# Mean-centred squares on one core: four 4 MB loads on one queue and stores on another, changed to two 8 MB loads with row-by-row computation and all stores on the loads' queue

## The chip, the cores and the metric

One core of one Trainium2 chip runs the program; the other cores are idle. The metric is the device time of one execution in microseconds, given as the median of several runs. A profile's own span is some 1.8 us shorter than this time (82.9 against 84.65 us before the change), so spans are compared with spans and times with times.

## The reference

```python
def reference(x, axis):                 # x: 1024 x 4096 float32, axis -1
    mean = np.mean(x, axis=axis, keepdims=True)
    return ((x - mean) ** 2).astype(np.float32)
```

Every row needs its whole mean before its first output can be computed. 16.78 MB are read and 16.78 MB written.

## The kernel before

The 1024 rows are four tiles of 128 partitions with two rows each. All four tiles have their own buffer, so no load ever waits for one.

Some terms. DVE (VectorE) sums the rows and ACT (ScalarE) squares them; SP (SyncE) computes nothing here and only issues transfers (DMAs). A transfer goes into the queue of the engine that issues it, and both queues use the same 16 DMA engines. A *run* is the contiguous stretch that a transfer moves for one partition: 32 KiB for two rows, 64 KiB for four. A *packet* is one record of a DMA engine in the profile; apart from small ones, here it is one run. The *turn* is the moment when the loads end and the stores take over.

```python
Q = 2
x_t = x.rearrange("(n p q) d -> n p (q d)", p=P, q=Q)
out_t = out.rearrange("(n p q) d -> n p (q d)", p=P, q=Q)
for i in range(ntiles):                                   # 4 tiles
    x_tile = pool.tile([P, Q * D], mybir.dt.float32)
    nc.sync.dma_start(out=x_tile, in_=x_t[i])             # L40: SP's queue, 32 KiB per partition
    x_tiles.append(x_tile)
for i in range(ntiles):
    x_tile = x_tiles[i].rearrange("p (q d) -> p q d", q=Q)
    # ... neg_sum, neg_mean: [P, Q] ...
    nc.vector.reduce_sum(out=neg_sum, in_=x_tile, axis=X, negate=True)            # L47
    nc.vector.tensor_scalar_mul(out=neg_mean, in0=neg_sum, scalar1=inv_d)         # L53
    for q in range(Q):
        nc.scalar.activation(out=x_tile[:, q, :], in_=x_tile[:, q, :],
                             func=Square, bias=neg_mean[:, q:q + 1], scale=1.0)   # L56
    nc.scalar.dma_start(out=out_t[i], in_=x_tiles[i])     # L63: ACT's queue
```

(Cuts: imports, the pools, the launch.) A scheduler fixes the order of each engine's instructions at build time, and it need not be the order of the source.

## Time and profile before

| | before |
|---|---|
| time, median | 84.65 us |
| span of the profile | 82.9 us |
| DVE, ACT busy | 43%, 37% of the span |
| packets of the two DMA queues, share of 16 engines' span | 48.6% + 47.0% |
| bytes over the span | 405 GB/s |

How to read it: the last two rows say that the 16 DMA engines are the bound. The packets themselves took 95.6% of 82.9 us, which is 79.25 us; in the other 3.65 us an average DMA engine had no packet.

The groups of instructions of the kernel before (columns: busy us and mean ns of one, then idle time ahead of them and what ended it) show where the two arithmetic engines stand:

```profile
L47 DVE TENSOR_REDUCE neg_sum<-x_tile 128x2 f32<-128x8192 f32 x4 | 34.7, 8686 | 25.6 <-DMA x_tile<-in_x_dram 25.6
L56 ACT ACTIVATE x_tile<-x_tile,neg_mean 128x4096 f32<-128x4096 f32 x8 | 29.2, 3700 | 24.9 <-DVE neg_mean L53 24.9
```

Both are idle for about 25 us while they wait for data or for each other. Neither is the bound.

### The profile page before, as it was taken

To read this page: it belongs to the slowest core of one execution; us is meant where nothing else is said; L and a number is where in the kernel's file an instruction comes from. 1 tells how busy PE (TensorE), PEld (TensorE's weight loads), DVE (VectorE), ACT (ScalarE), POOL (GpSimd) and SP (SyncE) were. 2 spreads that over 40 slices of the span, in tenths; PEclk is the share of its full clock that TensorE was granted. 3 is DMA by queue.
4 is the path that set the end of the run, shared out by engine and by line. 5 is a ranking of instruction groups with operands and counts; after the bars stand their busy time and mean duration, and the time that the engine had idled before them with its cause. 6 is when DMAs were issued, how large, how long until landed. Compare 5 with 4: busy or idle time off the path is not lost.

```text
span 82.9 us, 75 instructions
## 1 busy us (share of the span) xinstructions
DVE 35.4 (43%) x8; ACT 30.5 (37%) x9; POOL 0.2 (0%) x4
## 2 busy tenths in 40 slices
DVE  0000007999599995999900000799950000000000
ACT  0000006000399917998099950000049990000000
POOL 0000000000000000000000000000000000000000
DMA  7779997997999899997997999899796996995990
GB/s 190 300 332 443 506 427 332 506 490 316 459 506 411 348 506 285 443 474 316 490 490 332 443 490 427 348 506 474 332 443 285 506 490 269 506 506 253 506 506 0
DMA packets 1153, 33.55 MB, mean 405 GB/s; under 512 B 129, under 2 KB 129, under 8 KB 129
## 3 DMA queue, kind: packets, MB, share of 16 engines
q1 hardware_dynamic: 576, 16.78, 48.6%
q10 hardware_dynamic: 576, 16.78, 47.0%
q14 instruction: 1, 0.00, 0.0%
HBM read 16.78 MB, written 16.78 MB: 405 GB/s over the span
## 4 chain that ended last, share of the span: by engine, by line
DMA 37%; DVE 21%; another core or an unknown queue 13%; ACT 5%; issue 4%; SPq 1%
DMA x_tile<-in_x_dram 37%; DVE neg_sum L47 21%; ACT x_tile L56 5%; SPq L40 1%; DVE neg_mean L53 0%
## 5 line engine op out<-in xcount | busy, mean ns | idle before, releaser
L47 DVE TENSOR_REDUCE neg_sum<-x_tile 128x2 f32<-128x8192 f32 x4 | 34.7, 8686 | 25.6 <-DMA x_tile<-in_x_dram 25.6
L56 ACT ACTIVATE x_tile<-x_tile,neg_mean 128x4096 f32<-128x4096 f32 x8 | 29.2, 3700 | 24.9 <-DVE neg_mean L53 24.9
L56 ACT ACT_TABLE_LOAD x1 | 1.3, 1283 | 13.1 <-DMA x_tile<-in_x_dram 13.1
L53 DVE TENSOR_SCALAR neg_mean<-neg_sum 128x2 f32<-128x2 f32 x4 | 0.7, 170 | 0.1
L80 POOL MEMSET const-bfloat16-1.0<- 128x1 bf16 x1 | 0.1, 102 | 0.0
L80 POOL MEMSET const-uint8-127<- 128x1 uint8 x1 | 0.1, 102 | 0.0
L80 POOL MEMSET const-float32-1.0<- 128x1 f32 x1 | 0.1, 99 | 0.0
L80 POOL MEMSET const-float32-0.0<- 128x1 f32 x1 | 0.1, 98 | 0.2 <-issue 0.2
## 6 DMA issues: line engine op xcount, KB each, us to landing
x_tile<-in_x_dram SPq DMA_DIRECT2D x4, 4096.0 KB, 26.2
out_dram<-x_tile ACTq DMA_DIRECT2D x4, 4096.0 KB, 17.4
```

Source lines behind the costliest of these rows:

```text
L40: nc.sync.dma_start(out=x_tile, in_=x_t[i])
L47: nc.vector.reduce_sum(out=neg_sum, in_=x_tile, axis=mybir.AxisListType.X, negate=True,)
L53: nc.vector.tensor_scalar_mul(out=neg_mean, in0=neg_sum, scalar1=inv_d)
L56: nc.scalar.activation(out=x_tile[:, q, :], in_=x_tile[:, q, :], func=mybir.ActivationFunctionType.Square, bias=neg_mean[:, q:q + 1], scal ...
L80: nc = _bacc.Bacc("TRN2", target_bir_lowering=False, num_devices=1)
```

## The change

Its intent: fewer and longer loads (64 KiB per partition instead of 32), outputs that leave two rows at a time so that a large tile need not be finished before its first store, and one issuing queue, SP's, for everything.

```diff
-    Q = 2
+    Q = 4
+    H = 2
...
     for i in range(ntiles):                 # 2 tiles now
         for q in range(Q):
-        nc.vector.reduce_sum(out=neg_sum, in_=x_tile, ...)        # both rows at once
-        nc.vector.tensor_scalar_mul(out=neg_mean, in0=neg_sum, scalar1=inv_d)
-        for q in range(Q):
-            nc.scalar.activation(..., bias=neg_mean[:, q:q + 1])
-        nc.scalar.dma_start(out=out_t[i], in_=x_tiles[i])
+            row = tiles[i][:, q * D:(q + 1) * D]
+            nc.vector.reduce_sum(out=neg_sum, in_=row, ...)        # one row
+            nc.vector.tensor_scalar_mul(out=neg_mean, in0=neg_sum, scalar1=inv_d)
+            nc.scalar.activation(out=row, in_=row, ..., bias=neg_mean)
+            if q % H == H - 1:
+                part = slice((q + 1 - H) * D, (q + 1) * D)
+                nc.sync.dma_start(out=out_t[i][:, part], in_=tiles[i][:, part])
```

(Condensed; the loads' code is the same with Q = 4. H is the number of rows per store.)

More of the change, by code (lines that the diff above doesn't have):

```diff
@@ L10 @@
 from concourse._compat import with_exitstack
+F32 = mybir.dt.float32
 @with_exitstack
@@ L32 @@
     out_t = out.rearrange("(n p q) d -> n p (q d)", p=P, q=Q)
-    pool = ctx.enter_context(tc.tile_pool(name="io", bufs=ntiles))
-    stats = ctx.enter_context(tc.tile_pool(name="stats", bufs=ntiles))
-    x_tiles = []
+    io = ctx.enter_context(tc.tile_pool(name="io", bufs=ntiles))
+    stats = ctx.enter_context(tc.tile_pool(name="stats", bufs=2 * ntiles * Q))
+    tiles = []
     for i in range(ntiles):
-        x_tile = pool.tile([P, Q * D], mybir.dt.float32)
+        x_tile = io.tile([P, Q * D], F32)
         nc.sync.dma_start(out=x_tile, in_=x_t[i])
-        x_tiles.append(x_tile)
+        tiles.append(x_tile)
     for i in range(ntiles):
-        x_tile = x_tiles[i].rearrange("p (q d) -> p q d", q=Q)
-        neg_sum = stats.tile([P, Q], mybir.dt.float32)
-        neg_mean = stats.tile([P, Q], mybir.dt.float32)
-        nc.vector.reduce_sum(
-            out=neg_sum,
-            in_=x_tile,
-            axis=mybir.AxisListType.X,
-            negate=True,
-        )
-        nc.vector.tensor_scalar_mul(out=neg_mean, in0=neg_sum, scalar1=inv_d)
-        for q in range(Q):
+        for q in range(Q):
+            row = tiles[i][:, q * D:(q + 1) * D]
+            neg_sum = stats.tile([P, 1], F32)
+            neg_mean = stats.tile([P, 1], F32)
+            nc.vector.reduce_sum(
+                out=neg_sum, in_=row, axis=mybir.AxisListType.X, negate=True
+            )
+            nc.vector.tensor_scalar_mul(out=neg_mean, in0=neg_sum, scalar1=inv_d)
             nc.scalar.activation(
-                out=x_tile[:, q, :],
-                in_=x_tile[:, q, :],
+                out=row,
+                in_=row,
                 func=mybir.ActivationFunctionType.Square,
-                bias=neg_mean[:, q:q + 1],
+                bias=neg_mean,
                 scale=1.0,
             )
-        nc.scalar.dma_start(out=out_t[i], in_=x_tiles[i])
+            if q % H == H - 1:
+                part = slice((q + 1 - H) * D, (q + 1) * D)
+                nc.sync.dma_start(out=out_t[i][:, part], in_=tiles[i][:, part])
 _INS = ['x', 'axis']
```

## The prediction

> **What bounds the kernel now.** I read the page top down: busy shares, then the DMA row and the queues.
>
> ```profile
> DVE 35.4 (43%) x8; ACT 30.5 (37%) x9; POOL 0.2 (0%) x4
> ...
> DMA  7779997997999899997997999899796996995990
> ...
> q1 hardware_dynamic: 576, 16.78, 48.6%
> q10 hardware_dynamic: 576, 16.78, 47.0%
> ...
> HBM read 16.78 MB, written 16.78 MB: 405 GB/s over the span
> ```
>
> The arithmetic engines are each busy under half of the span. The DMA row is 7 to 9 tenths almost from the first slice to the last, and the two queues (q1 the loads, q10 the stores) together hold the 16 DMA engines for 48.6 + 47.0 = 95.6% of it. So the bound is moving 33.55 MB. The chain of waits names DMA 37% and DVE 21%, but that chain follows semaphores; a transfer that queues behind another leaves no semaphore event, so I trust the DMA row.
>
> What matters, then, is where the DMA engines run below their best rate. I cut the span into stages at the moments when transfers land or are issued (columns: window, its length, busy time of DVE, ACT and POOL, clock, DMA share, GB/s).
>
> ```profile
> 1.00:3.40 2.40, 0.00 (x0) 0.00 (x0) 0.00 (x0) 1.00 0.80 218
> 3.40:22.80 19.40, 8.90 (x3) 2.12 (x2) 0.00 (x0) 1.00 1.00 432
> 22.80:29.30 6.50, 6.50 (x1) 6.47 (x2) 0.00 (x0) 1.00 1.01 439
> 29.30:41.40 12.10, 11.17 (x4) 7.32 (x3) 0.00 (x0) 1.00 1.01 412
> 41.40:52.30 10.90, 0.03 (x1) 7.30 (x2) 0.00 (x0) 1.00 1.00 433
> 52.30:61.20 8.90, 8.83 (x2) 0.01 (x1) 0.00 (x0) 1.00 0.96 416
> 61.20:62.00 0.80, 0.00 (x0) 0.80 (x1) 0.00 (x0) 1.00 0.01 0
> 62.00:81.00 19.00, 0.00 (x0) 6.50 (x2) 0.00 (x0) 1.00 1.03 442
> ```
>
> Loads alone run at 432 GB/s, loads beside stores at 433 once settled. There are three weak places. The start-up up to 3.4 us; the stage in which the first store joins the loads (412 instead of 432); and a true hole, 61.20 to 62.00, where nothing moves. The timeline tells what the hole is:
>
> ```profile
> 45.00 3.69 ACT L56 ACTIVATE x_tile<-x_tile,neg_mean 128x4096 f32<-128x4096 f32 x1
> 61.20 3.71 ACT L56 ACTIVATE x_tile<-x_tile,neg_mean 128x4096 f32<-128x4096 f32 x1 [12.50 <-DVE neg_mean L53]
> 61.20 0.34 ACTq L63 DMA_DIRECT2D out_dram<-x_tile  x1
> ```
>
> The third tile was finished at 45.00 + 3.69 = 48.69, but its store is issued at 61.20: the scheduler put that DMA behind the next tile's first ACTIVATE in ACT's stream, and this ACTIVATE waits 12.50 us for the last mean. By 61.2 the second store has drained and the DMA engines run dry.
>
> **What the Trainium skill says.** (1) "DMA: Bandwidth & Descriptors", Where 436 GB/s comes from: 16 ports x 32 B x 850 MHz give 435 GB/s. The trace agrees, 432 to 433 in the settled stages, so longer runs have almost nothing to win there. (2) The same page, Queues, rings and completion order: each DMA engine takes descriptors of one ring in order, and takes turns between rings by packet. The stores joining at 29.3 while the loads are unfinished fit this; in-order within one queue, on which my estimate of the change rests, no part of this trace shows. (3) "VectorE: DVE Perf Modes", The perf-mode tier table: tensor_reduce runs at one element a cycle, at 0.96 GHz. 8192 elements are 8533 ns; the trace has 8686, so 153 ns is fixed per instruction. (4) "ScalarE: Activation LUTs", What ACT_TABLE_LOAD costs: 280 ns + 0.833 ns per element with a pointer bias, 3692 ns for 4096; the trace has a mean of 3700.
>
> **The change, part by part.**
>
> *Loads.* Two of 8.39 MB for four of 4.19 MB, same queue, same bytes. Load 0 lands when tile 1 lands now: the reduction that waited for it starts at 22.75. Load 1 lands 8.39 MB later: at 432 GB/s that is 19.4 us, so at 42.2, if no store gets between. All stores now stand behind the loads on the same queue, so none should. DVE has no work until 22.75 instead of 13.04; that costs nothing by itself as long as stores are ready when the loads end.
>
> *Is store 0 ready?* A one-row reduction is 4096/0.96 + 153 = 4420 ns (estimate from the row above). The compiled order is reduce, reduce, scale, reduce, scale, reduce, scale, scale: the first mean comes after two reductions. From 22.75: two reductions to 31.6, scale (0.17) to 31.8, ACTIVATE row 0 to 35.5; meanwhile the third reduction ends at 36.25, the second scale at 36.45, ACTIVATE row 1 runs 36.5 to 40.2. Store 0 is issued at 40.2. The first bytes came some 0.85 us after an issue (store issued 61.20, hole over by 62.0 to 62.1), so at 41.1. Load 1 finishes its data a little before its waiter starts at 42.2; tile by tile the engines finish over about half a microsecond. So store 0 is ready just in time, with 0 to 1 us to spare.
>
> *Store 1*: fourth reduction to 40.9, last scales to 41.25, ACTIVATEs from 41.1 to 48.4; issued at 48.4, well ahead of store 0's end (41.7 + 9.7 = 51.4).
>
> *Store 2*: the same computation from 42.2: issued 17.45 us later at 59.6, bytes possible from 60.5. Stores 0 and 1 need 19.4 us from 41.7, so to 61.1. In time by 0.6 us. *Store 3* is issued at 59.6 + 8.2 = 67.8, store 2 drains at 70.8: hidden.
>
> *The end.* Each DVE and ACT piece is hidden, so the sum is start-up plus bytes. The landing behind the 22.75 start was some 0.3 us earlier, so 22.4; after it 25.17 MB at 432 GB/s take 58.3 us: the last store lands at 80.7. Now it lands at about 81.7 (last store issued at 68.53; the four issue-to-landing times have minimum 11.2, median 17.4, maximum 23.7, which leaves 13.2 for this one). Up to 1.0 us is gained. Counted the other way, by what is removed: the hole, 0.8 us, and the stage at 412 for 432, 12.1 x (1 - 412/432) = 0.55 us, 1.3 us in all. Against this stands one new event: the DMA engines go from pure loading to pure storing at about 41.5. The one start-up I can see, the first 1.9 us for a round that later takes 1.2, lost 0.7 us; I allow 0.4 us for the turn.
>
> *Removed and added instructions*: four more reductions x 153 ns = 0.6 us of DVE, four more scales x 0.17 = 0.7 us; all on an engine with half its time free. No more packets than now in the stores; loads of 64 KiB runs may halve theirs, worth at most (435 - 432)/435 of the load time, 0.3 us.
>
> Sum: 84.68 - 1.15 (mean of the two counts) + 0.4 = 83.9 us.
>
> **The rivals.** (a) *Hidden anyway, no gain*: the turn at 41.5 costs a full restart (0.7 us) and store 2 comes late by up to 0.5 us: 84.7 to 85.0. For it: both margins are under a microsecond and hang on a reduction time I scaled, not measured. (b) *A wait takes the hole's place*: if the one-row reduction costs clearly more than 4.42 us, each tile loses this on two or three reductions before its first store, twice; 0.5 us each would open gaps of about 1 us at 41.5 and at 61: 85.5 to 86. Against it: 8686 ns for exactly twice the elements leaves little room. (c) *The bound itself moves*: 64 KiB runs put the DMA engines' concurrent streams at twice the distance in HBM; a loss of 3% on the loads would cost 1.2 us, giving 85.1. Nothing in the trace speaks for it or against. (d) *Better*: no turn cost and full rate: 83.3 or slightly less. DVE or ACT becoming the bound is ruled out: each stays under 38 us of 83.
>
> **Range and chances.** Centre **83.9 us**, range **83.1 to 85.1**: the lower end is (d) with a few tenths of packet gain, the upper end (a) or (c). Faster by over 2% means under 83.0, more than hole and weak stage together return net: 7%. Slower by over 2% means above 86.4, both new gaps at over 1 us: 4%. Within 2%: 89%.
>
> **What would show each step.** The first reduction starts at about 22.75 and lasts about 4420 ns; the fifth starts at about 42.2 (later means slow 64 KiB loads or a store between). SP issues stores at about 40.2, 48.4, 59.6 and 67.8. The windows should show no zero stretch near 61, and at 41 to 43 at most 0.4 us of dip; a hole at either place means that a margin failed. Span 82.1 for 82.9. I am wrong if the settled rate is not 432, or if stores on the loads' queue do not start promptly behind them.

## The result, and the profile after

The changed kernel takes **83.16 us** (83.12 to 83.20, 4 runs) against 84.65 us (84.6 to 84.7, 4 runs). The ratio is 0.9826 (95% interval 0.9812 to 0.9840), a gain of 1.7%; ratios here are the mean time of one kernel's fast runs over the mean time of the other's in the same rounds, so not quite the ratio of the medians. The gain is far outside the noise and below 2%.

First the page of the changed kernel: busy shares, the queue, and the groups.

```profile
DVE 35.4 (44%) x16; ACT 30.7 (38%) x9; POOL 0.2 (0%) x4
...
q1 hardware_dynamic: 864, 33.55, 96.2%
...
L51 DVE TENSOR_REDUCE neg_sum<-x_tile 128x1 f32<-128x4096 f32 x8 | 35.0, 4413 | 24.1 <-DMA x_tile<-in_x_dram 24.1
L55 ACT ACTIVATE x_tile<-x_tile,neg_mean 128x4096 f32<-128x4096 f32 x8 | 29.4, 3704 | 13.5 <-DVE neg_mean L54 13.5
```

The packets now take 96.2% of 81.3 us, which is 78.2 us, and 3.1 us are idle. Of the 1.6 us that the span lost, about 1.05 us are shorter packets (79.25 to 78.2) and about 0.55 us less idle time (3.65 to 3.1). (The shares are rounded, so both parts are good to about 0.1 us.) The bytes are the same, so the first part is a surprise: something made packets take longer before.

The stages by windows (columns as in the prediction: window, its length, busy time of DVE, ACT and POOL, clock, DMA share, GB/s), cut so that the turn from loads to stores and the place of the old hole stand alone:

```profile
3.40:22.80 19.40, 0.30 (x1) 0.25 (x1) 0.00 (x0) 1.00 1.00 432
...
40.60:41.80 1.20, 0.00 (x0) 1.20 (x1) 0.00 (x0) 1.00 1.02 437
41.80:43.00 1.20, 1.17 (x1) 1.20 (x1) 0.00 (x0) 1.00 1.01 437
...
60.00:61.20 1.20, 0.00 (x0) 1.20 (x1) 0.00 (x0) 1.00 1.02 437
61.20:62.00 0.80, 0.00 (x0) 0.80 (x1) 0.00 (x0) 1.00 1.14 492
```

There is no hole near 61 us, and no dip where loads give way to stores. A word on this view: it books a packet's whole time and bytes to the window in which the packet starts (shares above 1 come from this). So in a window in which each engine starts exactly one packet, **share times window length is the time of one packet**: here 1.02 x 1.20 = 1.22 us for 32 KiB. I use this below.

The same word corrects a reading of the prediction. It calls 61.20 to 62.00 of the kernel before "a true hole", "where nothing moves". The window shows only that no packet *starts*. The trace also keeps every packet with its start and duration; followed engine by engine, these packet records show that the packets begun before it end between 61.27 and 62.36 us, and that the next ones start at 62.04 to 62.17 us, or at once on the last engine. So the 16 engines were idle for 0.60 us on average, not for 0.8.

The timeline shows the starts: of the reductions, and of the four stores (one line for a group of four).

```profile
22.50 8.75 DVE L51 TENSOR_REDUCE neg_sum<-x_tile 128x1 f32<-128x4096 f32 x2 [22.50 <-DMA x_tile<-in_x_dram]
...
39.46 27.65 SPq L64 DMA_DIRECT2D out_dram<-x_tile  x4
...
41.83 8.75 DVE L51 TENSOR_REDUCE neg_sum<-x_tile 128x1 f32<-128x4096 f32 x2 [1.62 <-DMA x_tile<-in_x_dram]
```

Taken singly, the stores are issued at 39.46, 47.45, 58.79 and 66.78 us, and the last takes 13.8 us to land, at 80.6 us. Before, the last store took 13.5 us from its issue at 68.53, so it landed at 82.0 us.

Then the same view of the kernel before, around the moment when its first store (issued at 29.30) meets the loads:

```profile
30.20:31.40 1.20, 1.20 (x1) 0.00 (x0) 0.00 (x0) 1.00 1.02 437
31.40:32.50 1.10, 0.25 (x3) 0.82 (x1) 0.00 (x0) 1.00 1.56 477
32.50:33.60 1.10, 1.10 (x1) 1.10 (x1) 0.00 (x0) 1.00 0.79 298
```

From 31.40 to 33.60 packets of 2.2 us x mean 387 GB/s = 0.85 MB began and took (1.56 + 0.79) x 1.10 = 2.59 us per engine; at 432 GB/s they would have taken 1.97 us. So here, once, packets were lengthened by 0.6 us per engine. That is most of the 1.05 us. The question for the experiments is what lengthens them: the second queue, the length of the runs, or something else.

### The profile page after: what moved, and what is told of

The parts are those of the page before. It is cut to its first block, busy times and chain, and to the rows that moved or that the text cites. A ratio compares the mean times of both kernels' runs of the same rounds, so it can differ in the third digit from the quotient of the medians.

```text
span 81.3 us, 79 instructions
## 1 busy us (share of the span) xinstructions
DVE 35.4 (44%) x16; ACT 30.7 (38%) x9; POOL 0.2 (0%) x4
## 3 DMA queue, kind: packets, MB, share of 16 engines
q1 hardware_dynamic: 864, 33.55, 96.2%
## 4 chain that ended last, share of the span: by engine, by line
DMA 50%; DVE 22%; ACT 5%; ACTq 4%; SPq 0%; issue 0%
DMA x_tile<-in_x_dram 50%; DVE neg_sum L51 21%; ACT x_tile L55 5%; ACTq L95 4%; SPq L43 0%; DVE neg_mean L54 0%
## 5 line engine op out<-in xcount | busy, mean ns | idle before, releaser
L51 DVE TENSOR_REDUCE neg_sum<-x_tile 128x1 f32<-128x4096 f32 x8 | 35.0, 4413 | 24.1 <-DMA x_tile<-in_x_dram 24.1
L55 ACT ACTIVATE x_tile<-x_tile,neg_mean 128x4096 f32<-128x4096 f32 x8 | 29.4, 3704 | 13.5 <-DVE neg_mean L54 13.5
L54 DVE TENSOR_SCALAR neg_mean<-neg_sum 128x1 f32<-128x1 f32 x8 | 1.1, 148 | 0.0
```

The lines of the kernel that those rows point to most:

```text
L51: nc.vector.reduce_sum(out=neg_sum, in_=row, axis=mybir.AxisListType.X, negate=True)
L55: nc.scalar.activation(out=row, in_=row, func=mybir.ActivationFunctionType.Square, bias=neg_mean, scale=1.0,)
```

## The experiments

All kernels gave correct results. Each was timed in turn with the kernel before, whose medians in the four calls were 84.72, 84.75, 84.67 and 84.73 us; a difference of 0.1 us between kernels of different calls says nothing.

### First: queue, run length, hole

My theory before these runs was the prediction's: the gain is the hole plus the joining of the second queue plus a little at the start. The rival was the longer runs of the loads.

**e1, the kernel before with its stores on SP's queue**

```diff
-        nc.scalar.dma_start(out=out_t[i], in_=x_tiles[i])
+        nc.sync.dma_start(out=out_t[i], in_=x_tiles[i])
```

> The kernel before, with its four stores moved from ACT's queue to SP's; loads stay four of 32 KiB runs, computation in pairs of rows. Theory (the gain of 1.49 us is the hole near 61 us, some 0.75, plus the loss where the second queue joins, some 0.5, plus some 0.2 at the start from the larger loads): 83.35 us. Rival (the longer runs of the loads bring the gain): 84.65 us, as before.

Measured: 84.24 us, ratio 0.9940. A miss: only 0.5 us of 1.49 us, although there is now one queue and no hole. Its windows around the turn from loads to stores:

```profile
37.00:38.20 1.20, 1.20 (x1) 1.20 (x1) 0.00 (x0) 1.00 1.01 437
...
39.40:40.60 1.20, 1.20 (x1) 0.00 (x0) 0.00 (x0) 1.00 1.68 437
40.60:41.80 1.20, 0.69 (x2) 0.44 (x1) 0.00 (x0) 1.00 0.00 0
41.80:43.00 1.20, 0.16 (x1) 1.20 (x1) 0.00 (x0) 1.00 1.02 437
```

The packets of 37.00 took 1.01 x 1.20 = 1.21 us. The last load packets, begun in 39.40 to 40.60, took 1.68 x 1.20 = 2.02 us, and nothing could start in the window after. So the loss of about 0.8 us at the meeting of loads and stores is there **with a single queue too**: the second queue cannot be its only cause.

**e2, the changed kernel with its stores back on ACT's queue**

```diff
-                nc.sync.dma_start(out=out_t[i][:, part], in_=tiles[i][:, part])
+                nc.scalar.dma_start(out=out_t[i][:, part], in_=tiles[i][:, part])
```

> The changed kernel with its stores back on ACT's queue. The compiled order puts store 1 behind the first ACTIVATE of tile 1, which starts at 50.67 us; store 0 drains at about 51, so the theory expects a hole of 0.5 us there and a short meeting of the two queues near 41: 83.7 to 83.9 us. Rival (longer runs): 83.2 us, as the changed kernel.

Measured: 84.04 us, ratio 0.9917; 0.9 us slower than the changed kernel, and above what either theory expected. Store 1 was indeed held back to 50.81 us by the order of ACT's stream, as expected. But the turn was not free either:

```profile
38.20:39.40 1.20, 1.20 (x1) 1.20 (x1) 0.00 (x0) 1.00 2.02 874
39.40:40.80 1.40, 0.96 (x3) 0.72 (x2) 0.00 (x0) 1.00 0.00 0
40.80:42.00 1.20, 0.03 (x1) 1.20 (x1) 0.00 (x0) 1.00 1.54 437
```

The last 64 KiB load packets took 2.02 x 1.20 = 2.42 us, as in the changed kernel, but the first store packets on the other queue took 1.54 x 1.20 = 1.85 us instead of 1.21. That is 0.64 us, the larger part of the 0.9. (The late store 1 left the 16 engines idle for 0.16 us on average by the packet records, not the 0.5 us expected.) The first store was issued at 39.62 us and load 1's reduction started at 41.97, against 39.46 and 41.83 in the changed kernel: the same moment beside the loads. So a store that comes just in time **by the other queue** still costs, and the second queue is not cleared.

**e3, the kernel before with the queues swapped**

```diff
-        nc.sync.dma_start(out=x_tile, in_=x_t[i])
+        nc.scalar.dma_start(out=x_tile, in_=x_t[i])
...
-        nc.scalar.dma_start(out=out_t[i], in_=x_tiles[i])
+        nc.sync.dma_start(out=out_t[i], in_=x_tiles[i])
```

> The kernel before with the queues swapped: loads issued by ACT, stores by SP. Two queues still share the engines from 30 to 52 us, but store 2 is issued when it is ready (48.7 us), so the hole must go. Theory: 84.65 - 0.75 = 83.9 us, the hole alone. If the joining of the queues costs nothing, 83.35 us. Rival (longer runs): 84.65 us.

Measured: 84.27 us, ratio 0.9953 (0.9922 to 0.9983), with runs spread from 83.97 to 84.81; a miss, for the theory said 83.9. Two queues, no held-back store, and as fast as e1 within that spread. The gain is 0.1 to 0.7 us, about 0.4 on average. The profile is of a run of 84.78 us, one that gained nothing; it shows that the late issue is gone (61 to 62 us moved 492 GB/s instead of 33) and that the lengthened packets stay (share 1.62 in the window 31.30 to 32.50, so 1.94 us).

**e4, the changed kernel with four loads of 32 KiB runs**

```diff
-    Q = 4
+    Q = 2
```

> The changed kernel with four loads of two rows (32 KiB runs) instead of two of four; row by row, stores on SP. Theory: 83.35 us, equal to the kernel before with stores on SP; the 64 KiB runs are worth 0.2 us. Rival (longer runs): 84.65 us.

Measured: 84.22 us, ratio 0.9935; as far from the expected 83.35 as e1, and equal to e1, so row by row instead of in pairs changes nothing there. Its last load packets were lengthened as in e1:

```profile
37.20:38.40 1.20, 1.20 (x1) 1.20 (x1) 0.00 (x0) 1.00 1.01 437
...
39.70:40.90 1.20, 1.20 (x1) 0.00 (x0) 0.00 (x0) 1.00 1.57 437
```

That is 1.57 x 1.20 = 1.88 us. Taken alone, e4 against the changed kernel (84.22 against 83.16) would say that 64 KiB runs are worth 1 us. But the two differ in one more thing: with four loads the first tile lands early, and its store is issued at 29.3 us and waits some 11 us behind the loads; in the changed kernel the first store is issued at 39.46 us, just before the loads end.

### Second: how late the first store may be

**e5, the changed kernel with its reductions in pairs of rows**

```diff
-        for q in range(Q):
-            row = ...                                  # one reduction, scale, ACTIVATE per row
+        for h in range(Q // H):
+            pair = ...                                 # one reduction and scale per two rows
```

(Condensed.)

> The changed kernel with the reductions in pairs of rows as before (two tiles, stores on SP). The compiled order runs both paired reductions of a tile before its first scale, so the first mean comes at 22.5 + 17.4 = 39.9 us and store 0 is issued at 47.4, first bytes at 48.2 instead of 41.2. Theory (only a late store costs): 7 us more, 90.1 us. Rival (row by row changes nothing that sets the end): 83.2 us.

Measured: 90.23 us, ratio 1.0642, as the theory expected; the first store was issued at 47.36 us. So row by row is needed with large tiles, not for its own speed but because the compiled order runs two reductions ahead of the first mean, and two paired ones take 17.28 us.

**e6 and e7, the changed kernel with a spare reduction ahead of tile 0's rows**

```diff
+        if i == 0:
+            spare = stats.tile([P, 1], F32)
+            nc.vector.reduce_sum(out=spare, in_=tiles[0][:, 0:W], axis=X)    # W = 1024 (e6), 4096 (e7)
```

> The changed kernel with one spare reduction of 1024 elements (1.22 us) ahead of tile 0's rows, its result unused. It moves store 0's issue from 39.46 to 40.7 and its bytes to about 41.55; the DMA engines end the loads between 40.96 and 41.47. Theory: a gap of 0.1 to 0.6 us, 83.3 to 83.8 us. Rival (stores queue behind loads with more slack than that): 83.2 us; rival (no slack at all): 84.4 us.

> The same with a spare reduction of 4096 elements (4.41 us). Bytes of store 0 at about 44.7. Theory: 4.41 - 0.9 = 3.5 us more, 86.7 us; no slack: 87.6 us; DVE's time hidden anyway: 83.2 us.

Measured: 83.64 us (e6) and 86.82 us (e7), both as the theory said. In e7 the store was issued at 43.90 us, 4.44 us later than in the changed kernel, which costs 3.66 us; so the slack of the first store in the changed kernel is about 0.8 us (4.44 - 3.66). In e6 the store was issued at 40.81 us, and the engines waited for it:

```profile
38.20:39.40 1.20, 1.20 (x1) 1.20 (x1) 0.00 (x0) 1.00 2.02 874
...
41.00:41.50 0.50, 0.50 (x3) 0.04 (x1) 0.00 (x0) 1.00 0.02 0
41.50:42.50 1.00, 0.52 (x2) 1.00 (x1) 0.00 (x0) 1.00 1.22 524
```

The load packets took their normal 2.42 us, but no data packet starts between 41.00 and 41.50.

**e8, an attempt to beat the changed kernel**

```diff
+        if i == 0:
+            nc.sync.dma_start(out=x_tile[:, :half], in_=x_t[i][:, :half])
+            nc.scalar.dma_start(out=x_tile[:, half:], in_=x_t[i][:, half:])
```

(Here and in e10 to e12 the other loads stay as they were.)

> An attempt to beat the changed kernel: its first load is cut in two by rows, one half issued by SP and the other by ACT at the same moment, so that two sequencers feed the DMA engines at the start. Theory: the start-up of some 0.7 us is mostly the first fetch, which this does not shorten: 83.2 us, at best 83.0. Rival (the start-up is issue time): 82.8 us.

Measured: 83.51 us, ratio 0.9851; no faster, and 0.35 us behind the changed kernel. It missed both expected values. Tile 0 was not there earlier but later: its first reduction starts at 22.73 us for 22.50. What the start-up consists of, which the theory took for a fetch, no run here shows. The turn of this kernel is used below.

### Third: how early the first store may be

New theory A, after e1 to e4: a store that already waits behind the loads lengthens the last load packets; one issued just before the loads end does not. Rival B: the 64 KiB runs make the turn free.

**e9, e4 with its first store delayed to the changed kernel's moment**

```diff
+            for w in (Q * D, 1250):        # in e4, ahead of tile 0's rows: 10.05 us of spare reductions
+                nc.vector.reduce_sum(out=spare, in_=tiles[0][:, 0:w], axis=X)
```

> Four loads of 32 KiB runs, row by row, stores on SP (the kernel of 84.22 us), plus two spare reductions (10.1 us of DVE, results unused) that move the first store's issue from 29.3 to about 39.5 us, which is where the changed kernel issues it. In the kernel of 84.22 us the last load packets before the turn to stores took about 2.0 us instead of 1.21. Theory A (a store that waits in the queue behind the loads lengthens the turn; one issued just before it does not): 83.2 to 83.4 us, no long packets. Theory B (the 64 KiB runs of the last load make the turn free, whenever the store is issued): 84.2 us, long packets again.

Measured: **83.66 us**, ratio 0.9877: adding 10 us of useless work on DVE made e4 0.56 us *faster*. Its windows at the same place as e1's:

```profile
37.00:38.20 1.20, 1.20 (x1) 1.20 (x1) 0.00 (x0) 1.00 1.01 437
38.20:39.40 1.20, 1.20 (x1) 1.20 (x1) 0.00 (x0) 1.00 1.01 437
39.40:40.60 1.20, 1.20 (x3) 0.52 (x2) 0.00 (x0) 1.00 1.01 437
40.60:41.80 1.20, 1.20 (x1) 1.20 (x1) 0.00 (x0) 1.00 1.02 437
```

Every window holds one packet of 1.21 to 1.22 us; the long packets are gone. The time is a little above the expected 83.2 to 83.4. The store was issued at 39.84 us, where I had aimed at 39.5. It is 0.5 us slower than the changed kernel, and run length is only a small part of that. By the packet records a 64 KiB packet takes 2.418 us against twice 1.213, which is 0.12 us over the 16 packets of each engine. The rest is store packets (1.220 us on average instead of 1.213, so 0.2 us), idle time at the turn (0.09 us) and engines that end less evenly.

**e10, the changed kernel with its first load in two parts, so that the first store comes early**

```diff
+        if i == 0:                          # both on SP
+            nc.sync.dma_start(out=x_tile[:, :half], in_=x_t[i][:, :half])
+            nc.sync.dma_start(out=x_tile[:, half:], in_=x_t[i][:, half:])
```

> The changed kernel with its first load cut into two of two rows, both on SP; the second load stays one of 64 KiB runs. The first store is then issued at about 29.3 us and waits some 11 us behind the loads. Theory A (an early store lengthens the turn): 84.0 us. Theory B (64 KiB runs make the turn free): 83.2 us.

Measured: 84.43 us, ratio 0.9963; 1.27 us slower than the changed kernel. Its last load still has 64 KiB runs, so B is refuted (that the cut of the first load is not to blame is shown below), and the loss is even larger than A's number:

```profile
35.80:38.20 2.40, 0.00 (x0) 2.40 (x1) 0.00 (x0) 1.00 1.02 437
38.20:39.40 1.20, 0.00 (x0) 0.52 (x1) 0.00 (x0) 1.00 3.18 874
39.40:41.80 2.40, 0.00 (x0) 0.00 (x0) 0.00 (x0) 1.00 0.00 0
```

The last load packets took 3.18 x 1.20 = 3.82 us, the ones ahead of them 1.02 x 2.40 = 2.45 us.

**e11 and e12, e10 with its first store delayed by spare reductions of 7.03 and 8.85 us**

```diff
+            for w in (6600,):               # e11;  (8192, 100) in e12
+                nc.vector.reduce_sum(out=spare, in_=tiles[0][:, 0:w], axis=X)
```

> The kernel of e10 with a spare reduction of 7.03 us that moves the first store's issue from 29.0 to about 36.8 us. The last load packets start at about 38.6 to 39.1 us and, undisturbed, end near 41.0 to 41.6; the store's descriptors then wait in the queue before the last packets start. Theory (the last load packet is lengthened when a store already waits at its start): long packets again, 84.4 us. Rival (only a wait of many microseconds lengthens it): 83.2 us.

> The same with spare reductions of 8.9 us, first store issued at about 38.6 us, its descriptors at the DMA engines some 0.85 us later, after the last load packets have started and some 1.5 us before they end. Theory: no long packets and no gap, 83.2 us, as the changed kernel (issue at 39.46). Rival (any store that waits costs): 83.8 to 84.4 us.

Measured: 84.62 us (e11, ratio 0.9985) and 83.90 us (e12, ratio 0.9901). In e12, issue at 38.51 us:

```profile
38.20:39.40 1.20, 1.05 (x3) 0.52 (x2) 0.00 (x0) 1.00 2.61 874
```

So e12 missed: I expected a free turn once the last packets had started, and they were still lengthened, by about half as much as in e10. My threshold is wrong; the table shows what holds in its place. The seven kernels with everything on one queue and measured packets at the turn:

| kernel | runs of the last load | first store issued | last load packets | lengthened by | time |
|---|---|---|---|---|---|
| e1 | 32 KiB | 29.27 | 2.02 us | 0.8 us | 84.24 |
| e4 | 32 KiB | 29.32 | 1.88 us | 0.7 us | 84.22 |
| e9 | 32 KiB | 39.84 | 1.21 us | none | 83.66 |
| e10 | 64 KiB | 29.03 | 3.82 us | 1.4 us | 84.43 |
| e11 | 64 KiB | 36.74 | 3.96 us (share 3.30 x 1.20) | 1.5 us | 84.62 |
| e12 | 64 KiB | 38.51 | 3.13 us | 0.7 us | 83.90 |
| changed | 64 KiB | 39.46 | 2.42 us | none | 83.16 |

The times follow the lengthening: e10, e11 and e12 lie 1.27, 1.46 and 0.74 us above the changed kernel, for 1.40, 1.54 and 0.71 us. An early store lengthens the last load packets by some 0.6 of their own time, whichever their length (0.7 to 0.8 of 1.21 us, 1.4 to 1.5 of 2.42 us). In e12, where the store came latest of the five, it was 0.3.

One rival is left for e10 to e12: they also have their first load in two parts. e8 has the same two parts (one by ACT's queue) and its first store late, at 39.69 us. Its turn:

```profile
38.20:39.40 1.20, 1.20 (x1) 1.20 (x1) 0.00 (x0) 1.00 2.02 874
```

The last load packets took 2.42 us, not lengthened, so the cut does not do it. Why the DMA engines lengthen packets no run here shows.

## Why the prediction was right or wrong

The time fell inside the range, but only just: 83.16 us for a centre of 83.9 and a low end of 83.1, and the gain, 1.49 us, was about twice that of its sum. Point by point:

- **Bound and hole: right, but the hole was taken too large.** The DMA engines stay the bound, and the hole at 61.20 is gone because no store is behind ACT's waiting ACTIVATE any more. It was worth 0.60 us and not 0.8, since the window view hides packets under way. e3, which removes the late issue and keeps two queues, gains about 0.4 us.
- **Computation times: right.** A one-row reduction takes 4413 ns on average for 4420 predicted. The fifth reduction starts at 41.83 for 42.2, and the stores are issued at 39.46, 47.45, 58.79 and 66.78 us for 40.2, 48.4, 59.6 and 67.8: all 0.7 to 1.0 us early. 0.25 us of this is load 0's earlier landing. Much of the rest is that instructions follow each other a little faster than I added them up: the first scale starts at 31.16, 8.66 us after the first reduction, where I had counted 8.84 us.
- **Margins: right in kind.** I gave store 0 "0 to 1 us to spare"; e7 measures about 0.8 us. Stores behind loads on one queue started promptly.
- **The end: right by one count, mis-sized in the sum.** "The last store lands at 80.7" came out at 80.6. But I set the old landing at 81.7, from a 13.2 us guessed out of minimum, median and maximum; asked for singly, that store took 13.5 us and landed at 82.0. The gain by this count was 1.4 us, not 1.0. To the mean of two counts I then added **0.4 us for the turn** from loading to storing. It cost nothing: the windows at 40.60 and 41.80 run at 437 GB/s. These two terms, 0.4 us and half of another 0.4, explain most of the 0.7 us between prediction and result; what came true is rival (d), "no turn cost and full rate: 83.3 or slightly less".
- **The weak stage "412 instead of 432": size right, cause only half right.** I put it down to the second queue. e1 keeps the loss with one queue, because its first store is early; e2 has it with a late first store, because it has two queues. It is a single event, in which packets are lengthened where stores meet loads. The kernels without it (the changed one, e6, e8 and e9) have both one queue for loads and stores at the turn and a first store that comes late enough. The change meets the second condition by luck: the prediction saw a danger in a late store and none in an early one.
- **Rivals (a), (b), (c): not what happened.** No restart cost, no new gap, and loads with 64 KiB runs at 432 GB/s as before.

What the prediction's parts came to can be added up from the packet records of the two profiles, per DMA engine. Packets are 0.96 us shorter in sum: 0.67 at the meeting of loads and stores, 0.12 from the 64 KiB runs, 0.11 from store packets that took 1.220 us after the hole and 1.213 without it, 0.06 from the first packets. Idle time between the first and the last packet falls by 0.64 us, of which 0.60 is the hole. The start (first packet at 1.74 and 1.75 us) and the end (1.16 and 1.15 us after the last packet) are the same. That makes 1.6 us for the 1.5 us between the spans before rounding, 82.88 and 81.35 us, so the sum closes to 0.1 us.

Left open: the mechanism of the lengthening, and how general the cost of the second queue is: e2 is the only run with two queues and a late first store. No run beat the changed kernel, and between e12 (38.51, too early) and e6 (40.81, too late) its 39.46 us sits in a window of at most 2.3 us that nothing in the source protects.

## What to carry to other kernels

In a kernel bound by DMA, compare the sum of packet time with the idle time before blaming either: here nearly two thirds of the gain came from shorter packets, and only about 0.6 us from idle time, where I had looked first. A window without packet starts is not yet an idle window. Look at the first store's issue against the end of the loads: too late leaves a gap, but a store queued long before costs too, and here delaying it with useless work made a kernel faster. The free turn was seen only with loads and stores on one queue. And find where the scheduler put each DMA issue in its engine's stream; a store behind an instruction that waits is late however early its data was ready.

## What the Trainium skill lacked or had wrong

- "DMA: Bandwidth & Descriptors" (Queues, rings and completion order; Rules for kernel authors) has no cost for turning from loads to stores. The runs show that the last load packets take 1.88 to 2.02 us for 1.21 us (32 KiB) and 3.13 to 3.96 us for 2.42 us (64 KiB) when a store already waits behind them, and 2.42 us as usual in the changed kernel, whose store is issued about 0.8 us earlier than it has to be. When that store comes by the other queue (e2), its first packets take 1.85 us instead of 1.21.
- The same page's rule "Overlap DMA with compute" says to issue early and names no exception. For this kernel an earlier first store was slower: 84.43 us issued at 29.03 us, 83.90 us at 38.51 us, 83.16 us at 39.46 us (the last with its first load in one piece).
- The same page (Specifications) gives a first-byte latency of about 0.6 us for DMAs issued from SP, and does not say from which moment. In e5, e6 and e7, where DMA engines had run dry, the first packet of the store starts 0.84 us after the start of the issuing instruction (48.20 for 47.36, 41.65 for 40.81, 44.74 for 43.90), which is 0.5 us after the end of that instruction.
